# A two-layer decoder trunk: a value unit with three seven-product pairs, a key norm and the gates at later steps

## The chip, the cores and the metric

The kernel runs on one core of a Trainium2 chip. The core has TensorE (matrix products, "PE" in the profile, its weight loads "PEld"), VectorE ("DVE"), ScalarE ("ACT"), GpSimd ("POOL") and SyncE ("SP", which issues the transfers). TensorE's products go to eight PSUM banks of 128 x 512 float32; everything else lies in on-chip SBUF, and weights come from HBM. The metric is the device time of one execution in microseconds; the median of the runs is compared.

## The reference

Two layers. In each, one projection of the normed input feeds eight heads of gated linear attention (GLA) and eight heads of stick-breaking attention, whose outputs are projected back; then a squared-ReLU MLP. Sequence 256, model width 2048, float32.

```python
def hybrid_layer(x, attn_norm, w_in, w_gate_up, b_gate, gla_out_norm,
                 sb_q_norm, sb_k_norm, sb_out_norm, w_o, mlp_norm, w_up, w_down):
    h = rms_norm(x, attn_norm)
    proj = jnp.einsum('bsd,de->bse', h, w_in)
    g_q, g_k, g_v, g_gate, g_lr, s_q, s_k, s_v = jnp.split(proj, COL_SPLITS, axis=-1)
    gate_logits = jnp.einsum('bsr,re->bse', g_lr, w_gate_up) + b_gate
    log_a = jax.nn.log_sigmoid(gate_logits.astype(jnp.float32)) / GLA_GATE_TAU
    o_gla = gla_chunked(split_heads(g_q, GLA_HEADS), split_heads(g_k, GLA_HEADS),
                        split_heads(g_v, GLA_HEADS), split_heads(log_a, GLA_HEADS))
    ...
    sq = rms_norm(split_heads(s_q, SB_HEADS), sb_q_norm)
    sk = rms_norm(split_heads(s_k, SB_HEADS), sb_k_norm)
    o_sb = stick_breaking_attention(sq, sk, split_heads(s_v, SB_HEADS))
    ...
    x = x + jnp.einsum('bse,ed->bsd', mixed, w_o)
    hm = rms_norm(x, mlp_norm)
    up = jnp.square(jax.nn.relu(jnp.einsum('bsd,df->bsf', hm, w_up)))
    return x + jnp.einsum('bsf,fd->bsd', up, w_down)
```

## The kernel before

**Products in three parts.** A float32 operand is split into a high part in the reduced type float32r and a low part (the rest). A product is the sum of high x high, high x low and low x high, three matmuls on TensorE. For weights, ScalarE makes the high half (`whi`) and VectorE subtracts it from the raw weights for the low half (`wlo`); for some weights the low half is made by ScalarE and an adding transfer of GpSimd's queue (`dlo`). A raw weight tile is 1 MB and comes on SP's queue.

**A layer has two stretches.** The first is the attention (lines 811 to 1081), traced in program order and ordered by the framework. Its work is cut into units of 512 (or fewer) output columns (`unit`, line 565, and the transposed `unit_t`, line 611). Each half group of a unit's weights is followed by a call of `tick` (line 365). `after(n, fn)` (line 362) files a piece of work, and the n-th tick from then runs it, so that small pieces of TensorE's and VectorE's work are laid between the units' products. One tick is called a step below: 12 matmuls of 512 columns in `unit`, eight of 512 and eight of 256 in `unit_t`. `tick` also puts the pieces behind the newest high and low parts on their engines.

The second stretch (from line 1085) is an order written out by a planner, `Plan` (line 42): every piece has an engine, a length, predecessors, and a due time counted back from TensorE's order; VectorE and ScalarE take the piece that is due first. It holds the second gate unit ("g"), the output projection ("o"), the MLP ("up", "down"), and, in layer 1, two units of layer 2's projection, 1024 columns each: "iv" for the stick-breaking values and "ik" for the keys. They leave `natural["iv"]` and `natural["ik"]`, two tiles each, the second of which is needed by the second four heads.

**Seven-product pairs.** A unit of the planner has eight pairs of 128 weight rows, by 1024 columns. With two row tiles of the sequence and two column halves, a pair is a 2 x 2 block product. `FAST` (line 24) names the pairs that are done with seven block products in place of eight (1, 3, 5 and 6): VectorE makes sums of weight blocks (line 1097, three instructions, into `ts` and back into `raw`), sums of the operand's blocks are made once per operand pair (`forms`, line 422), and the pair has four steps (21 matmuls of 512 columns) in place of two (24). `STEPS` (line 22) is the order of the steps of a unit: the same pair number stands in it once for each step. `unit_order` (line 1109) returns both, `step_banks` (line 1119) gives the PSUM banks of each step, `steps` (line 1300) makes the weight parts. Pairs 2 and 7 (`ADDED`) take their low halves by the adding transfer.

**Layer 2's attention around the change.** The order of units is: low-rank gate columns with two query heads (line 881), the short query unit of two heads (`ub`, line 948), the long query unit of four heads (`uq`, line 964), then the GLA query and key units of `unit_t`. Steps are counted from the end of `ub`: steps 1 to 8 are `uq`, 9 to 12 the first GLA query unit, 13 to 16 the second. The pieces are:

- `sb_qk` (line 659), a norm: `head_sums` (line 642) squares a row tile and reduces it over each head (lines 645, 646), one step later `finish` does the second row tile, the inverse root, and `mul_heads` (line 651); `wait` steps after the call, `turn` transposes two heads on TensorE (line 688), and VectorE copies the result (line 695, or 697 for queries), and again one step later for two more heads. For the second key norm the input is `natural["ik"][1]`, which is normed in place.
- `sb_heads` (line 849): for the first four heads, scores at steps 2 and 6, weights (line 742) three steps and outputs (line 754) four steps later. For the second four heads, called when `uq` has ended (step 8), scores at steps 14 and 18.
- `gates` (line 903): two calls. Each has four small matmuls (line 911), ScalarE and VectorE work, a small copy on GpSimd, and three GpSimd products (line 945).

Of the kernel before, what the change touches and what calls it, by code (L numbers as in the profile page):

```python
# [21 lines left out]
STEPS = [0, 0, 1, 1, 1, 2, 3, 1, 3, 2, 3, 3, 4, 4, 5, 5, 6, 5, 5, 6, 6, 6, 7, 7]  # L22
LOADS = [0, 1, 2, 3, 4, 5, 6, 7]
FAST = (1, 3, 5, 6)
ADDED = (2, 7)
BIG = ("up", "down", "iv", "ik")
DEPTH = 2
# [117 lines left out]
def trunk_kernel(  # L145
# [51 lines left out]
    def act_tile(dt, shape=(P, 4, T)):  # L197
        return apool.tile(list(shape), dt, tag="act", name=nm("act"))

    def ps_tile():  # L200
        return pools["ps"].tile([P, 512], F32, tag="ps", name=nm("ps"))
# [8 lines left out]
    def tmp(tag, shape, dt=F32, bufs=2):  # L210
        pool = pools["att"] if tag in ATT else pools["mlp"] if tag in MLP else tpool
        return pool.tile(list(shape), dt, tag=tag, name=nm(tag), bufs=bufs)
# [20 lines left out]
    def stat(n):  # L233
        return spool.tile([P, n], F32, tag=f"st{n}", name=nm("st"))
# [127 lines left out]
    def after(n, fn):  # L362
        held.append((clock[0] + n, fn))
# [31 lines left out]
    def inv_rms(ss, n, width):  # L395
        rr, parts = inv_rms_parts(ss, n, width)
        for part in parts:
            part()
        return rr
# [19 lines left out]
    def fast(i):  # L419
        return i in FAST  # L420

    def forms(op, i, t, tag):
# [18 lines left out]
        def high():  # L441
            if e:
                if keep:
                    op.x[i] = act_tile(F32R, (P, 4, 2, P))
                else:
                    op.x[i] = tmp(tag, [P, 3, 2, P], F32R, bufs=len(FAST))
                todo.append((op.x[i], e[0]))
# [194 lines left out]
    def head_sums(ss, src, nh):  # L642

        sq = tmp("t2", [P, 512], bufs=T2)
        nc.vector.tensor_tensor(sq[:, : nh * P], src, src, ALU.mult)
        nc.vector.tensor_reduce(
            ss, sq[:, : nh * P].rearrange("p (h d) -> p h d", d=P), AX.X, ALU.add
        )

    def mul_heads(dst, src, rr, nh):  # L650
        nc.vector.tensor_tensor(
            dst.rearrange("p (h d) -> p h d", d=P),
            src.rearrange("p (h d) -> p h d", d=P),
            rr.unsqueeze(2).to_broadcast([P, nh, P]),
            ALU.mult,
        )


    def sb_qk(acc, c, nh, h0, rst, scale, dst, wait, nat=None):

        w = nh * P
        made = nat is None
        nat = act_tile(F32, (P, NT, 512)) if made else nat
        ss = stat(NT * nh)

        def part(tt):
            if made:
                nc.scalar.activation(
                    nat[:, tt, :w], acc[:, tt, c : c + w], AF.Copy, scale=rst[:, tt : tt + 1]
                )  # L670
            head_sums(ss[:, tt * nh : (tt + 1) * nh], nat[:, tt, :w], nh)

        def finish():
            part(1)
            rr = inv_rms(ss, NT * nh, P)
            for tt in range(NT):
                mul_heads(
                    nat[:, tt, :w], nat[:, tt, :w], rr[:, tt * nh : (tt + 1) * nh], nh
                )

        part(0)
        after(1, finish)

        def turn(h):
            pt = ps_tile()
            for j in range(2):
                for tt in range(NT):
                    nc.tensor.transpose(  # L688
                        pt[:, j * T + tt * P : j * T + (tt + 1) * P],
                        nat[:, tt, (h + j) * P : (h + j + 1) * P], ident,  # L690
                    )
            d = dst[:, h0 + h : h0 + h + 2, :]
            s = pt.rearrange("p (h t) -> p h t", t=T)
            if scale is None:
                nc.vector.tensor_copy(d, s)
            else:
                nc.vector.tensor_scalar(d, s, scale, None, ALU.mult)

        for i, h in enumerate(range(0, nh, 2)):
            after(wait + i, lambda h=h: turn(h))  # L700
# [86 lines left out]
    def values(acc, v):  # L787
        for tt in range(NT):
            nc.scalar.activation(
                v[:, tt, :], acc[:, tt, :], AF.Copy, scale=st["rst"][:, tt : tt + 1]  # L790
            )
        return v
# [18 lines left out]
    for l in range(DEPTH):  # L811
# [60 lines left out]
        if l == 0:  # L872
            uk = unit(hT, wl, 0, C_SK, 512)
            rst = st["rst"]
            kT = act_tile(F32)
            sb_qk(uk, 0, 4, 0, rst, None, kT, 4)
        else:
            rst = st["rst"]
            kT = act_tile(F32)
# [23 lines left out]
        def gates(b):  # L903
            if b == 0:
                gt["e"] = [act_tile(F32) for _ in range(3)]
                gt["dec"] = tmp("dec", [P, 4, 4], bufs=1)
            eb, enb, ekd = gt["e"]
            pl = ps_tile()
            for e in range(2):
                ee = 2 * b + e  # L910
                nc.tensor.matmul(
                    pl[:, e * T : (e + 1) * T], kc["wg"][:, ee * P : (ee + 1) * P], gt["lrT"],
                    start=(e == 0), stop=True, skip_group_check=True,
                )
            a = tmp("t2", [P, 512], bufs=T2)
            nc.scalar.activation(a, pl, AF.Abs)
            nc.scalar.activation(a, a, AF.Exp, scale=-1.0)
            nc.scalar.activation(a, a, AF.Ln, bias=1.0)
            nc.vector.scalar_tensor_tensor(a, pl, 0.0, a, ALU.min, ALU.subtract)
            bc = tmp("t2", [P, 512], bufs=T2)  # L920
            for e in range(2):
                es = slice(e * T, (e + 1) * T)
                nc.vector.tensor_tensor_scan(
                    bc[:, es], kc["reset"], a[:, es], 0.0, ALU.mult, ALU.add
                )
            bs = slice(2 * b, 2 * b + 2)

            def fl(t):
                return t[:, bs, :].rearrange("p e t -> p (e t)")

            nc.scalar.activation(fl(eb), bc, AF.Exp, scale=1.0 / GATE_TAU)
            nc.scalar.activation(fl(enb), bc, AF.Exp, scale=-1.0 / GATE_TAU)
            bc3 = bc.rearrange("p (n c) -> p n c", c=CHUNK)
            nc.vector.tensor_tensor(
                a.rearrange("p (n c) -> p n c", c=CHUNK),
                bc3[:, :, CHUNK - 1 : CHUNK].to_broadcast([P, 8, CHUNK]), bc3, ALU.subtract,
            )
            nc.scalar.activation(fl(ekd), a, AF.Exp, scale=1.0 / GATE_TAU)
            nc.gpsimd.tensor_copy(
                gt["dec"][:, bs, :],  # L940
                eb[:, bs, :].rearrange("p e (n c) -> p e n c", c=CHUNK)[:, :, :, CHUNK - 1],
            )
            rb = gt["row"].unsqueeze(1).to_broadcast([P, 2, T])
            for t in (eb, enb, ekd):
                nc.gpsimd.tensor_tensor(t[:, bs, :], t[:, bs, :], rb, ALU.mult)
# [3 lines left out]
        sb_qk(ub, 0, 2, 2, rst, gqk[:, l : l + 1], qT, 3)  # L949
        sb_heads(0, qT, kT, v, (2, 6))  # L950
        for b in range(2):
            after((9 if l == 0 else 1) + 2 * b, lambda b=b: gates(b))

        if l == 0:
            uv = unit(hT, wl, 0, C_SV + 512, 512)
            v = values(uv, tmp("v4", [P, NT, 512], bufs=2))
            uk = unit(hT, wl, 0, C_SK + 512, 512)
            kT = act_tile(F32)
            sb_qk(uk, 0, 4, 0, rst, None, kT, 4)
        else:  # L960
            v = natural["iv"][1]
            kT = act_tile(F32)
            after(4, lambda kT=kT: sb_qk(None, 0, 4, 0, rst, None, kT, 3, natural["ik"][1]))
        uq = unit(hT, wl, 0, C_SQ + 512, 512)
        qT = act_tile(F32)
        sb_qk(uq, 0, 4, 0, rst, gqk[:, l : l + 1], qT, 3)
# [140 lines left out]
        natural = {}  # L1107

        def unit_order(u):

            kind, _, n2 = units[u]
            if kind == "g":
                return [i // 2 for i in range(8)], ()
            if kind == "o":
                pairs = ((4, 5, 6, 7, 0, 1, 2, 3), (4, 5, 6, 0, 7, 1, 2, 3))[n2]
                return [j for j in pairs for _ in range(4 if j < 2 else 2)], (0, 1)
            return STEPS, FAST

        def step_banks(u, j, is_fast):

            kind = units[u][0]
            if kind == "g":
                return (1, 6), (1, 6)
            if kind in BIG and j in ADDED and not by_columns(u, j):
                return ((2, 4, 3, 8),) * 2
# [120 lines left out]
        def by_columns(u, i):  # L1246

            return units[u][0] in BIG and i in ADDED and i == unit_order(u)[0][-1]

# [50 lines left out]
        def steps(u, j, is_fast, r, ld, readers):  # L1300
# [23 lines left out]
            if not is_fast:  # L1324
                added = kind in BIG and j in ADDED
                if added and not by_columns(u, j):
# [292 lines left out]
        gate(0)  # L1619
        for u, (kind, q, n2) in enumerate(units):  # L1620
            order, quick = unit_order(u)
            if kind != "g":
                tails[u] = (down_tail if kind in ("o", "down") else up_tail)(u)
# [94 lines left out]
```

## Time and profile before

| | |
|---|---|
| median of 3 runs | 2145.22 us (2144.92 to 2146.12) |
| the profiled execution, its own time | 2145.51 us |
| its span, first to last instruction | 2143.8 us |
| transfers | 480.37 MB, mean 224 GB/s |
| short query unit ends on TensorE | 1188.2 us of the span |
| long query unit ends (step 8) | 1221.6 us |
| scores of step 14 begin | 1242.85 us |

All times inside the kernel are counted from the span's start. In a view of the timeline a row has the start, the duration, the engine, the line, the operation, output <- input, sizes, the count, and in brackets how long the engine stood idle before it and what released it. The time between two starts of TensorE says more than the durations, since its products overlap: a matmul of 512 columns is drawn 0.39 us long, while the next one starts 0.23 us later. The view of waits gives, for each pair of lines, the total, the number and the longest of an engine's waits.

### The profile page before, as it was taken

Reading aid. Unit: us, or ns where it says so; the run is one execution under the profiler, and the core shown is the slowest. Engines: PE = TensorE matmul, PEld = TensorE weight load, DVE = VectorE, ACT = ScalarE, POOL = GpSimd, SP = SyncE. Lnnn points to the kernel's source line nnn. Section 1 sums busy time; section 2 is a strip of 40 time slices with the busy share of each in tenths; the row PEclk is TensorE's granted clock in tenths of the full one; section 3 lists DMA queues with packets and bytes.
Section 4 is the critical chain, followed back from the end, with each engine's and each line's share of the span. In section 5 each row is a group of like instructions: output and inputs, shape, how many; then the busy total and the mean of one; then the engine's idle time right before and its main releaser. Section 6 shows DMA issues by size and latency. Waiting matters only on the chain.

```text
span 2143.8 us, 28392 instructions
## 1 busy us (share of the span) xinstructions
PE 2134.1 (100%) x10239; PEld 1780.4 (83%) x10239; DVE 1892.3 (88%) x2533; ACT 1471.4 (69%) x1889; POOL 157.0 (7%) x210
## 2 busy tenths in 40 slices
PE   9999999999999999999999999999999999999999
PEld 7988888888888888888878888888888888888887
DVE  5677669999999999999998875799999999999998
ACT  5555456678677677678776654667876776776775
POOL 0020000000000000000001200000000000000000
PEclk9999999999999999999999999999999999999999
DMA  6655456688888888888886544657888888888886
GB/s 229 196 158 167 158 197 196 196 245 265 244 253 246 260 251 243 273 236 255 238 242 170 176 159 158 202 173 228 253 243 274 236 261 247 248 247 253 255 249 182
DMA packets 169105, 480.37 MB, mean 224 GB/s; under 512 B 9370, under 2 KB 34530, under 8 KB 168964
## 3 DMA queue, kind: packets, MB, share of 16 engines
q1 hardware_dynamic: 149380, 407.24, 56.4%
q0 software_dynamic: 19584, 71.31, 17.6%
q8 instruction: 80, 1.31, 0.2%
q14 instruction: 61, 0.50, 0.1%
HBM read 405.12 MB, written 2.10 MB: 190 GB/s over the span
## 4 chain that ended last, share of the span: by engine, by line
PE 94%; DVE 3%; issue 1%; ACT 1%; DMA 0%; POOL 0%; DVEq 0%; ACTq 0%
PE acc L577 4%; PE acc L579 4%; PE acc L578 4%; PE acc L624 3%; PE acc L628 1%; DVE wlo L1268 1%; DVE wlo L560 0%; DVE xb L1097 0%; PE ps L1065 0%; DMA raw<-in_w_in_dram 0%; PE ps L1058 0%; PE ps L742 0%; PE ps L1015 0%; PE ps L688 0%; PE ps L706 0%
## 5 line engine op out<-in xcount | busy, mean ns | idle before, releaser
L1264 ACT ACTIVATE whi<-raw 128x1024 fp32r<-128x1024 f32 (+1 forms) x768 | 738.9, 976 | 314.4 <-issue 45.3
L1268 DVE TENSOR_TENSOR wlo<-raw,whi 128x1024 fp32r<-128x1024 f32 (+1 forms) x632 | 689.1, 1097 | 65.6 <-ACT whi L1264 54.0
L560 DVE TENSOR_TENSOR wlo<-raw,whi 128x1024 fp32r<-128x1024 f32 (+2 forms) x162 | 182.2, 1131 | 93.3 <-ACT whi L558 93.2
L558 ACT ACTIVATE whi<-raw 128x1024 fp32r<-128x1024 f32 (+2 forms) x162 | 156.0, 968 | 153.4 <-PE acc L579 109.3
L1277 POOL DMA_DIRECT2D dlo<-raw x136 | 117.2, 862 | 1587.6 <-ACT dlo L1274 837.7
L1264 ACT ACTIVATE whi<-ts 128x1024 fp32r<-128x1024 f32 x144 | 152.7, 1061 | 73.6 <-DVE ts L1097 4.0
L577 PE MATMUL acc<-whi,act 128*128 128x512 f32 (+2 forms) x512 | 191.4, 374 | 0.0
L578 PE MATMUL acc<-wlo,act 128*128 128x512 f32 (+2 forms) x512 | 186.5, 364 | 0.1
L579 PE MATMUL acc<-whi,act 128*128 128x512 f32 (+2 forms) x512 | 186.5, 364 | 0.0
L1268 DVE TENSOR_TENSOR wlo<-ts,whi 128x1024 fp32r<-128x1024 f32 x144 | 175.5, 1219 | 10.2 <-ACT whi L1264 8.5
L1097 DVE TENSOR_TENSOR ts<-raw 128x1024 f32<-128x1024 f32 x144 | 175.6, 1220 | 1.6
L1274 ACT ACTIVATE dlo<-raw 128x1024 fp32r<-128x1024 f32 x136 | 139.0, 1044 | 3.6 <-PE m__1930_9320 L1378 1.7
L577 PEld LDWEIGHTS acc<-whi,act 128*128 128x128 f32 x512 | 96.7, 189 | 17.5 <-issue 2.7
L579 PEld LDWEIGHTS acc<-whi,act 128*128 128x128 f32 x512 | 96.4, 188 | 15.5
L578 PEld LDWEIGHTS acc<-wlo,act 128*128 128x128 f32 x512 | 96.6, 189 | 14.2 <-DVE wlo L560 0.6
L1097 DVE TENSOR_TENSOR raw<-raw 128x512 f32<-128x512 f32 x144 | 98.9, 687 | 2.3
L1097 DVE TENSOR_TENSOR raw<-ts,raw 128x512 f32<-128x512 f32 x144 | 98.6, 684 | 0.5
L624 PE MATMUL acc<-act,whi 128*128 128x512 f32 x256 | 91.9, 401 | 0.0
L628 PE MATMUL acc<-act,wlo 128*128 128x256 f32 x256 | 71.6, 280 | 0.0
L1469 ACT ACTIVATE act<-act,st 128x512 f32<-128x512 f32 x72 | 49.0, 712 | 19.2 <-DVE act L1097 19.2
L454 DVE TENSOR_TENSOR act<-t,act 128x512 fp32r<-128x512 f32 x84 | 57.0, 683 | 0.0
L624 PEld LDWEIGHTS acc<-act,whi 128*128 128x128 f32 x256 | 48.1, 188 | 10.7
(3145 smaller groups left out, 5333.1 us busy)
## 6 DMA issues: line engine op xcount, KB each, us to landing
raw<-in_w_up_dram SPq DMA_DIRECT2D x112, 1024.0 KB, 5.7
raw<-in_w_down_dram SPq DMA_DIRECT2D x112, 1024.0 KB, 5.9
raw<-in_w_in_dram SPq DMA_DIRECT2D x82, 1024.0 KB, 5.3
dlo<-raw POOLq DMA_DIRECT2D x136, 512.0 KB, 6.5
raw<-in_w_o_dram SPq DMA_DIRECT2D x32, 1024.0 KB, 5.1
raw<-in_w_up_dram SPq DMA_DIRECT2D x32, 512.0 KB, 6.3
raw<-in_w_down_dram SPq DMA_DIRECT2D x32, 512.0 KB, 6.5
raw<-in_w_in_dram SPq DMA_DIRECT2D x18, 512.0 KB, 5.9
```

What stands on the lines that cost most here:

```text
L558: newest["hi"] = nc.scalar.activation(h, r, AF.Copy).ins
L560: newest["lo"] = nc.vector.tensor_tensor(lo[:, q : q + step, :width], r, f32(h), ALU.subtract).ins
L577: nc.tensor.matmul(o, xh[:, sl], whi[:, j, :width], start=first, stop=False)
L578: nc.tensor.matmul(o, xh[:, sl], wlo[:, j, :width], start=False, stop=False)
L579: st["mm"] = nc.tensor.matmul(o, xl[:, sl], whi[:, j, :width], start=False, stop=last).ins
L624: nc.tensor.matmul(acc[:, f, :], whi[:, j, sl], op.both(k), start=(k == 0), stop=False, skip_group_check=True,)
L628: nc.tensor.matmul(acc[:, f, T:], wlo[:, j, sl], xh, start=False, stop=(k == KT - 1), skip_group_check=True,)
L1097: nc.vector.tensor_tensor(dst, a, b, op)
L1264: nc.scalar.activation(box["h"][:, :n], src(), AF.Copy)
L1268: nc.vector.tensor_tensor(box["l"][:, :n], src(), f32(box["h"][:, :n]), ALU.subtract)
L1274: nc.scalar.activation(box["l"], src(), AF.Copy, scale=-1.0)
L1277: nc.gpsimd.dma_start(f32(box["l"]), src(), accum_op=ALU.add)
```

## The change

Three edits, all for layer 1's unit "iv" and layer 2's attention.

```diff
+FEWER = [0, 0, 1, 1, 1, 2, 3, 1, 3, 2, 3, 3, 4, 4, 5, 5, 6, 6, 6, 6, 7, 7], (1, 3, 6)
...
         for b in range(2):
-            after((9 if l == 0 else 1) + 2 * b, lambda b=b: gates(b))
+            after((9 if l == 0 else 2) + 2 * b, lambda b=b: gates(b))
...
-            after(4, lambda kT=kT: sb_qk(None, 0, 4, 0, rst, None, kT, 3, natural["ik"][1]))
+            after(10, lambda kT=kT: sb_qk(None, 0, 4, 0, rst, None, kT, 2, natural["ik"][1]))
...
-            return STEPS, FAST
+            return FEWER if kind == "iv" else (STEPS, FAST)
```

In the unit "iv" the pairs 1, 3 and 6 have seven products; pair 5 is plain and has two steps, directly behind pair 4's, and pair 6's four steps follow one another. All other units of the planner, "ik" among them, keep `STEPS` and `FAST`, and `forms` still makes the operand's sums for pair 5, which "ik" reads. In layer 2, the second key norm begins at step 10 (it was 4), ends at step 11 (5), and turns its heads at steps 12 and 13 (7 and 8). The two calls of `gates` come at steps 2 and 4 (1 and 3); at step 2 they stand behind the scores of that step, which are filed first.

## The prediction

> **What bounds the kernel now.** I read the page first, then the waits of TensorE around the places that the diff touches, then those places instruction by instruction.
>
> ```profile
> span 2143.8 us, 28392 instructions
> PE 2134.1 (100%) x10239; PEld 1780.4 (83%) x10239; DVE 1892.3 (88%) x2533; ACT 1471.4 (69%) x1889; POOL 157.0 (7%) x210
> ```
>
> TensorE is busy for the whole span, so the time changes only by products added to or taken from it and by moments in which it waits. Between 980 and 1400 us (the end of layer 1 and the attention of layer 2) the view of waits, for TensorE, has three rows (total us, times, longest):
>
> ```profile
> PE ps L688 <- DVE act L651: 1.9, 2, 1.6
> PE m__2025_9760 L1378 <- DVE wlo L1268: 0.6, 1, 0.6
> PE m__2028_9771 L1378 <- DVE wlo L1268: 0.5, 1, 0.5
> ```
>
> All three waits are for VectorE, and all three lie where the diff works: L1268 makes the low halves for the value unit "iv", L651 ends the second key norm of layer 2. The stretches around them, engine by engine (PE, PEld, DVE, ACT, POOL busy us, each with its count):
>
> ```profile
> 1100.00:1116.00 16.00, 14.85 (x63) 11.24 (x62) 15.93 (x22) 12.16 (x17) 1.72 (x2) 1.00 0.89 239
> 1216.00:1222.00 6.00, 4.09 (x22) 3.17 (x21) 5.90 (x14) 4.54 (x7) 0.00 (x0) 1.00 0.89 286
> ```
>
> VectorE is full in both (15.93 of 16, 5.90 of 6) and TensorE is not. The granted clock is 1.00 in both, so these are waits, not a slower clock.
>
> **Part 1: pair 5 of the value unit becomes a plain pair.** The end of that unit on TensorE now, from pair 5's first product to pair 7's first:
>
> ```profile
> 1104.71 0.39 PE L1377 MATMUL m__2001_9660<-whi,act 128*128 128x512 f32 x1
> ...
> 1108.80 0.39 PE L1377 MATMUL m__2028_9771<-whi,act 128*128 128x512 f32 x1
> 1109.65 0.50 PE L1378 MATMUL m__2028_9771<-wlo,act 128*128 128x512 f32 x1 [0.46 <-DVE wlo L1268]
> ...
> 1111.60 0.40 PE L1377 MATMUL m__2025_9760<-whi,act 128*128 128x512 f32 x1
> 1112.59 0.50 PE L1378 MATMUL m__2025_9760<-wlo,act 128*128 128x512 f32 x1 [0.59 <-DVE wlo L1268]
> ...
> 1116.32 0.40 PE L1377 MATMUL m__2001_9660<-whi,act 128*128 128x512 f32 x1
> ```
>
> Between the first two rows lie three steps of six matmuls: 4.09 us / 18 = 0.227 us each, the undisturbed cadence. From 1104.71 to 1116.32 there are two seven-product pairs of 21 matmuls, 42 x 0.227 = 9.53 us, but the stretch takes 11.61: 2.08 us are lost. After the change it holds one plain pair (two steps x two banks x two blocks x three products, 24 matmuls) and one fast pair (21): 45 x 0.227 = 10.22 us. The three matmuls cost 0.68 us; if every wait goes, the stretch is 1.39 us shorter.
>
> Does every wait go? VectorE's groups between 1080 and 1120 us give the prices (the mean ns stands last before the idle column):
>
> ```profile
> L1268 DVE TENSOR_TENSOR wlo<-raw,whi 128x1024 fp32r<-128x1024 f32 x11 | 13.4, 1218 | 0.8 <-ACT whi L1264 0.8
> L1097 DVE TENSOR_TENSOR ts<-raw 128x1024 f32<-128x1024 f32 x4 | 4.9, 1218 | 0.0
> L1268 DVE TENSOR_TENSOR wlo<-ts,whi 128x1024 fp32r<-128x1024 f32 x4 | 4.9, 1216 | 0.0
> L1097 DVE TENSOR_TENSOR raw<-ts,raw 128x512 f32<-128x512 f32 x5 | 3.4, 683 | 0.0
> L1268 DVE TENSOR_TENSOR wlo<-raw,whi 128x512 fp32r<-128x512 f32 x4 | 2.7, 684 | 0.0
> L1097 DVE TENSOR_TENSOR raw<-raw 128x512 f32<-128x512 f32 x4 | 2.7, 683 | 0.0
> ```
>
> A fast pair takes the three weight sums (1.22 + 0.68 + 0.68) and four low parts (1.22 + 1.22 + 1.22 + 0.68): 6.9 us. A plain pair takes two low parts, 2.4 us. VectorE is relieved of 4.5 us, more than twice the 2.08 us by which it comes late, and pair 6, whose four steps now stand together (6.9 us of VectorE against 21 x 0.227 = 4.8 us of TensorE), has plain pairs 4 and 5 ahead of it (48 x 0.227 = 10.9 us of TensorE for 4.9 us of VectorE). So the waits should go. Ends: nothing gained and 0.68 us paid, or 1.39 us gained. I take 1.25, since behind 1109.98 the matmuls followed each other at 0.23 to 0.24 us even where nothing waited, and that may stay. What is not saved: the operand sums of pair 5 are still made, because the key unit "ik" keeps four fast pairs. Eight loads stay eight, ScalarE loses two high parts, no queue gets a new transfer. The ring of high tiles is two places further on when layer 2 begins; each place is freed in the same order, so I cost that at nothing.
>
> **Part 2: the second key norm leaves steps 4 to 8 behind the short query unit.** (A step is one tick, a half group of weights.) VectorE there:
>
> ```profile
> 1201.50 2.26 DVE L560 TENSOR_TENSOR wlo<-raw,whi 128x1024 fp32r<-128x1024 f32 x1 [0.87 <-ACT whi L558]
> ...
> 1207.66 0.67 DVE L645 TENSOR_TENSOR t<-act 128x512 f32<-128x512 f32 x1
> ...
> 1208.85 0.68 DVE L646 TENSOR_REDUCE st<-t 128x4 f32<-128x512 f32 x1
> 1209.44 1.47 DVE L645 TENSOR_TENSOR t<-act 128x512 f32<-128x512 f32 x1
> 1210.83 2.29 DVE L560 TENSOR_TENSOR wlo<-raw,whi 128x1024 fp32r<-128x1024 f32 x1
> 1213.05 0.67 DVE L646 TENSOR_REDUCE st<-t 128x4 f32<-128x512 f32 x1
> 1213.64 1.71 DVE L560 TENSOR_TENSOR wlo<-raw,whi 128x1024 fp32r<-128x1024 f32 x1
> ...
> 1216.49 0.16 DVE L389 TENSOR_TENSOR st<-st 128x8 f32<-128x8 f32 x1
> ...
> 1217.08 1.29 DVE L651 TENSOR_TENSOR act<-act,st 128x512 f32<-128x512 f32 x2
> ```
>
> And TensorE, which stands at the first transposes of that key tile:
>
> ```profile
> 1215.80 0.39 PE L579 MATMUL acc<-whi,act 128*128 128x512 f32 x1
> 1217.83 0.33 PE L688 MATMUL ps<-ident,act 128*128 128x128 f32 x1 [1.64 <-DVE act L651]
> ...
> 1218.73 0.47 PE L577 MATMUL acc<-whi,act 128*128 128x512 f32 x1
> ...
> 1221.57 0.60 PE L688 MATMUL ps<-ident,act 128*128 128x128 f32 x4
> 1221.92 0.48 PE L624 MATMUL acc<-act,whi 128*128 128x512 f32 x1
> ```
>
> The undisturbed block of four transposes takes 0.35 us (1221.57 to 1221.92). The disturbed one takes from 1215.80 + 0.23 to 1218.73, 2.70 us: 2.35 us lost. The norm's place is free of other necessity: its input was there since the end of layer 1, its result is first read by the scores of step 14. So this loss goes, and the eight transposes themselves (0.7 us) only change place.
>
> What comes late next is the question. The new place is steps 10 to 13, beside the norm of the long query unit:
>
> ```profile
> 1230.74 1.29 DVE L651 TENSOR_TENSOR act<-act,st 128x512 f32<-128x512 f32 x2
> ...
> 1234.61 0.74 DVE L697 TENSOR_SCALAR act<-ps,gqk 128x512 f32<-128x512 f32 x1
> ```
> ```profile
> 1233.07 0.60 PE L688 MATMUL ps<-ident,act 128*128 128x128 f32 x4
> 1236.33 0.60 PE L688 MATMUL ps<-ident,act 128*128 128x128 f32 x4
> ```
>
> That query norm ends at 1232.03, 1.04 us before step 11's turn (1233.07) needs it. The move takes from VectorE ahead of this point 0.67 + 0.68 + 1.47 + 0.67 + 1.29, four small instructions like L389 (0.16 each, 0.6) and the two copies behind the turns (0.74 each, by L697): 6.9 us. TensorE comes sooner by 2.35 + 0.70 = 3.05 us. If VectorE does all the key norm ahead of the query's, it takes on 0.67 x 4 + 0.6 + 1.29 = 4.6 us again: 1.04 + 6.9 - 4.6 - 3.05 = 0.3 us to spare. If it does the query's first, the key's turns at step 12 (behind 1236.33) meet a norm that ends about as late. That is close to even, and VectorE cannot bring all 6.9 us forward, because much of its work waits for TensorE's results. So a new wait in L688 has the ends 0 and the 2.35 us of the old one; I take 0.4, nearer the end that the ledger gives. Queued behind such a turn would be the rest of the first GLA query unit; VectorE's copies and the scores of step 14 wait for it. The moved step issues no transfer; SP's queue of weight loads keeps its order. Each turn needs one of four "ps" banks and step 14 two; the copies that free them (0.7 us) have a step of about 3.2 us (1233.07 to 1236.33). The natural key tile is held five steps longer and the key tile taken five steps later, so only steps 12 and 13 want one more of the 17 "act" buffers, when the query's natural tile is being freed.
>
> **Part 3: gates a step later.** Nothing is added: TensorE's gate products follow the scores of step 2 instead of going ahead of them. The result is first multiplied behind step 12, so the step is covered; without cover it would cost one step, 2.7 us (12 x 0.227). The six GpSimd products are moved with it:
>
> ```profile
> L945 POOL TENSOR_TENSOR act<-act,row x6: 1273/1453/2272, 1198.6 to 1212.0; 128x512 f32<-128x512 f32 x6
> ```
>
> Beside them the rows above show four VectorE instructions with two inputs in SBUF drawn out: 2.26, 2.29 and 1.71 instead of 1.22, and 1.47 instead of 0.67, in all 1.04 + 1.07 + 0.49 + 0.80 = 3.4 us. I take the same 3.4 us a step later, so nothing; ends are 0 and all six at 1.45 us, 8.7. The Trainium skill (SBUF — State Buffer, "Who interferes with whom") says that such a VectorE instruction and a GpSimd instruction that reads SBUF exclude one another, the later blocked to the end of the earlier. By that rule the worst is the end of 8.7 us, since any six instructions can be met; the rows so far show less than half of it.
>
> **Sum.** -1.25 - 2.35 + 0.4 = -3.2 us. The profiled execution took 2145.51 us (span 2143.8), 0.29 above the median of the runs, 2145.22. From its own time 2142.3, set against the median 2142.0.
>
> **Rivals.**
> - *Everything goes, the slow cadence too, and no new wait* (0.24): -1.39 - 2.35 = -3.74, 2141.5. For it: VectorE's relief of 4.5 us in part 1 is large; against it: the close ledger of part 2.
> - *The wait moves with the norm* (0.12): a new wait in L688 at step 12 of the old size, 2.35. Then only part 1 is left, 2145.22 - 1.25 = 2144.0. For it: VectorE's ledger leaves 0.3 us.
> - *The value unit doesn't gain* (0.08; the change does not do what it says): pair 6 alone still asks 6.9 us of VectorE for 4.8 us of TensorE, and if its parts are ordered late, 0.68 us are paid and waits of the old size stay: 0.68 - 2.35 + 0.4 = -1.3, 2143.9. Against it: 10.9 us of plain pairs ahead.
> - *Slower* (0.12): the GpSimd products, moved to steps 3 to 7, each hold a two-input VectorE instruction for their whole 1.45 us: 8.7 instead of 3.4 us, VectorE 5.3 us later. Less the 0.3 us to spare, step 11's turn waits 5.0 us instead of 0.4: -1.25 - 2.35 + 5.0 = +1.4, 2146.6. It decides as soon as that wait exceeds 3.6 us. It is the case that the skill's rule allows.
> - The forecast holds the rest, 0.44.
>
> **How the numbers follow.** The forecast's own range is 2141.3 to 2143.2. 2140.2 to 2145.2 holds the forecast, the first three rivals and the runs' scatter (2144.92 to 2146.12 before), and leaves out the slower one and a little below. 0.2% of 2145.2, about what a measurement can tell from no change, is 4.3 us: below 2140.9 or above 2149.5. My best case stops at 2141.5; that relief of VectorE gains something I do not see in its rows, part of the first rival and a little of the forecast, makes 0.18 for faster. Slower by 4.3 us needs a wait of 7.9 us in part 2: most of the slower rival's chance ends short of that, 0.08. Same: 0.74.
>
> **What would show it.** Right: TensorE's waits list between 980 and 1400 us without L1378 <- wlo and with L688 <- L651 under 1 us; about 10.2 to 10.4 us from pair 5's first product to pair 7's; L651 of the key norm ended before TensorE's second query turn. Wrong: a wait in L688 of 2 us or more near 1230 us, rows of L742 or L706 (scores) waiting for copies, low parts L1268 still late in pair 6, or VectorE instructions of over 2 us beside L945 in more than three places.

## The result, and the profile after

| | before | after |
|---|---|---|
| median of 22 runs each | 2145.97 us (2144.80 to 2147.50) | 2143.01 us (2142.38 to 2143.59) |
| the profiled execution, its own time | 2145.51 us | 2143.19 us |
| its span | 2143.8 us | 2141.5 us |

The ratio is 0.9986, with a 95% interval of 0.9979 to 0.9992: 0.14% faster, in the range 2140.2 to 2145.2 and, by the bound of 0.2%, "same". In the kernel after, every line behind line 25 has a number one higher: the norm's last step is L652, its transposes L689, the value unit's products L1378 and L1379. The head of the page of after:

```profile
span 2141.5 us, 28382 instructions
PE 2132.6 (100%) x10242; PEld 1779.8 (83%) x10242; DVE 1886.6 (88%) x2528; ACT 1470.5 (69%) x1887; POOL 158.4 (7%) x210
```

Three products more on TensorE, five instructions fewer on VectorE, two fewer on ScalarE: the edit of part 1. The waits of TensorE between 980 and 1400 us (total us, times, longest):

```profile
PE ps L689 <- DVE act L652: 0.8, 1, 0.8
PE m__2011_9701 L1379 <- DMA dlo<-raw: 0.3, 1, 0.3
```

The three old rows are gone (L688 1.9; L1378 0.6 and 0.5). Two new ones are there: a smaller wait of the transposes, and one for a low half that comes by an adding transfer. The timeline of TensorE in after, at both places:

```profile
1104.54 0.39 PE L1378 MATMUL m__2001_9660<-whi,act 128*128 128x512 f32 x1
...
1114.74 0.39 PE L1378 MATMUL m__2001_9660<-whi,act 128*128 128x512 f32 x1
...
1117.46 0.39 PE L1378 MATMUL m__2011_9701<-whi,act 128*128 128x512 f32 x1
1118.11 0.50 PE L1379 MATMUL m__2011_9701<-dlo,act 128*128 128x512 f32 x1 [0.26 <-DMA dlo<-raw]
...
1161.54 0.28 PE L578 MATMUL acc<-whi,act 128*128 128x272 f32 x1
...
1235.35 0.40 PE L625 MATMUL acc<-act,whi 128*128 128x512 f32 x1
1236.50 0.41 PE L689 MATMUL ps<-ident,act 128*128 128x128 f32 x2 [0.75 <-DVE act L652]
1236.74 0.38 PE L778 MATMUL ps<-ident,on 128*128 128x128 f32 x2
1237.01 0.87 PE L689 MATMUL ps<-ident,act 128*128 128x128 f32 x6
...
1240.15 0.59 PE L707 MATMUL ps<-act,act 128*128 128x256 f32 x2
```

In the value unit, pair 5's first product to pair 7's first (the first two rows) takes 10.20 us instead of 11.61: no wait is left in it, and no slow cadence. Behind it the product with `dlo` starts 0.65 us after the one ahead of it instead of 0.23: 0.42 us lost. At the key's turn, the last product starts at 1235.35 and the first transpose 1.15 us later instead of 0.23: 0.92 us lost. The framework put both turns of the key together here (eight transposes of L689), next to transposes of the output norm (L778).

Two fixed points cut the gain into three. Before they lie here, the first product of the low-rank unit and the scores of step 14:

```profile
1162.60 0.28 PE L577 MATMUL acc<-whi,act 128*128 128x272 f32 x1
...
1242.85 0.59 PE L706 MATMUL ps<-act,act 128*128 128x256 f32 x2
```

| stretch | before, us | after, us | difference |
|---|---|---|---|
| start to the low-rank unit | 1162.60 | 1161.54 | -1.06 (-1.41 in the value unit, +0.42 the `dlo` wait, -0.07 other) |
| low-rank unit to the scores of step 14 | 80.25 | 78.61 | -1.64 |
| the rest of the span | 900.95 | 901.35 | +0.40 |
| sum | 2143.8 | 2141.5 | -2.3 |

The middle stretch is the place of parts 2 and 3, and the measure for the experiments below: -2.35 for the old wait, +0.92 for the new one, and -0.2 elsewhere. From one execution to the next it moves by some tenths: two later profiles of the kernel before, with the same wait of the transposes, have 80.35 and 80.63.

### The profile page after: what moved, and what is told of

The parts are those of the page before. It is cut to its first block, busy times and chain, and to the rows that moved or that the text cites. A ratio compares the mean times of both kernels' runs of the same rounds, so it can differ in the third digit from the quotient of the medians.

```text
span 2141.5 us, 28382 instructions
## 1 busy us (share of the span) xinstructions
PE 2132.6 (100%) x10242; PEld 1779.8 (83%) x10242; DVE 1886.6 (88%) x2528; ACT 1470.5 (69%) x1887; POOL 158.4 (7%) x210
## 4 chain that ended last, share of the span: by engine, by line
PE 95%; DVE 2%; issue 1%; DMA 1%; ACT 1%; POOL 0%; ACTq 0%; DVEq 0%; POOLq 0%
PE acc L578 5%; PE acc L580 5%; PE acc L579 5%; PE acc L625 2%; PE acc L629 1%; DMA dlo<-raw 1%; DVE wlo L561 0%; DVE xb L1098 0%; PE ps L1066 0%; PE ps L1059 0%; DVE wlo L1269 0%; PE ps L689 0%; PE ps L1016 0%; PE ps L707 0%; PE ps L743 0%
## 5 line engine op out<-in xcount | busy, mean ns | idle before, releaser
L561 DVE TENSOR_TENSOR wlo<-raw,whi 128x1024 fp32r<-128x1024 f32 (+2 forms) x162 | 179.8, 1116 | 96.6 <-ACT whi L559 96.4
L1269 DVE TENSOR_TENSOR wlo<-ts,whi 128x1024 fp32r<-128x1024 f32 x143 | 174.4, 1220 | 10.2 <-ACT whi L1265 8.5
```

Source lines behind the costliest of these rows:

```text
L561: newest["lo"] = nc.vector.tensor_tensor(lo[:, q : q + step, :width], r, f32(h), ALU.subtract).ins
L1269: nc.vector.tensor_tensor(box["l"][:, :n], src(), f32(box["h"][:, :n]), ALU.subtract)
```

## The experiments

Each edit is shown against the kernel before unless said otherwise. All compute the same result: only the order of work and the number of seven-product pairs differ. Kernels of one group shared chip and runs of the kernel before. The ratio of a kernel to the kernel before stands with its 95% interval in brackets; where the interval reaches 1, the waits in the trace carry the argument, not the time.

**First group: each part by itself.** The kernel before had a median of 2145.92 us over 33 runs (2145.09 to 2148.03).

*Only the pairs* (with the line of `FEWER`, as in the change):

```diff
-            return STEPS, FAST
+            return FEWER if kind == "iv" else (STEPS, FAST)
```

> Only the value unit's edit (FEWER for iv), norm and gates as before. Theory, the three edits act in separate places and add up: the stretch from pair 5's first product to pair 7's is 10.2 us as in the changed kernel (11.6 before), the late dlo of pair 7 costs TensorE about 0.4 us there, and the 2.3 us in front of line 688/689's turn at step 7 stay, so about 1.0 us under the kernel before. Rival, the relief in the value unit gives VectorE a head start that also shortens the wait at step 7: about 2 us or more under before, with the step-7 wait clearly under 1.6 us.

Measured: 2144.98 us (2143.47 to 2146.46), ratio 0.9994 [0.9985, 1.0003], so -0.94. Its waits of TensorE in the same window:

```profile
PE ps L689 <- DVE act L652: 1.7, 2, 1.5
PE m__2011_9701 L1379 <- DMA dlo<-raw: 0.3, 1, 0.3
```

The waits for `wlo` are gone without the other parts, and the old wait of the transposes stays. What follows: part 1 takes its waits away alone, and the `dlo` wait belongs to it. The time agrees with the -1.0 expected, but the interval reaches over 1.

*Only the norm:*

```diff
-            after(4, lambda kT=kT: sb_qk(None, 0, 4, 0, rst, None, kT, 3, natural["ik"][1]))
+            after(10, lambda kT=kT: sb_qk(None, 0, 4, 0, rst, None, kT, 2, natural["ik"][1]))
```

> Only the second key norm's edit (start at step 10, turns at 12 and 13), pairs and gates as before. Theory: the 2.3 us at step 7 go, a new wait of about 0.9 us in front of the key's turn as in the changed kernel comes, so about 1.4 to 1.8 us under before; the gates' place does not matter. Rival, the gates' later step is what leaves VectorE free: with the gates at steps 1 and 3 the GpSimd products draw out 3.4 us of VectorE as before instead of the 1.5 to 2 of the changed kernel, the new wait is 2 us or more and the time is within 0.5 us of before.

Measured: 2143.41 us (2142.80 to 2144.50), 0.9988 [0.9979, 0.9997], so -2.5, more than I expected. Its waits:

```profile
PE m__2025_9760 L1378 <- DVE wlo L1268: 0.6, 1, 0.6
PE ps L742 <- DVE hl L731: 0.5, 1, 0.5
PE m__2028_9771 L1378 <- DVE wlo L1268: 0.4, 1, 0.4
```

No wait of the transposes is left in this view: with the gates in their old place the norm's move brings no new wait at the key's turn. The wait of L742 (TensorE's products for the attention weights) is no sign of the move: two later profiles of the kernel before have it too, 0.4 and 0.2 us.

*Only the gates:*

```diff
-            after((9 if l == 0 else 1) + 2 * b, lambda b=b: gates(b))
+            after((9 if l == 0 else 2) + 2 * b, lambda b=b: gates(b))
```

> Only the gates' edit (steps 2 and 4), pairs and key norm as before. Theory: the gates by themselves gain nothing, the key norm's wait at step 7 stays at 2 us or is longer by up to 1 us, since the gates' VectorE work now lies even nearer to it: within 1 us of before, not faster by more than 0.5. Rival: the VectorE instructions beside the GpSimd products are drawn out by 1.5 us less, and the wait at step 7 shrinks by that: 1 to 1.5 us under before.

Measured: 2149.46 us (2147.09 to 2150.12), 1.0015 [1.0006, 1.0024], so +3.5: a miss of mine. Its first wait:

```profile
PE ps L688 <- DVE act L651: 3.4, 1, 3.4
```

The old wait, 1.9 us in before, has grown by 1.5 us. The rest of the 3.5 goes with TensorE's clock (last section). Part 3 is not free: VectorE comes to the key norm later when the gates do.

*Norm and gates, the pairs as before:*

> Both edits of the attention, the value unit as before. Theory: additive, so the change (2.9 us under before) less the value unit's 1.0: about 1.9 us under before, with the new wait of 0.9 us at the key's turn and the waits of 0.6 and 0.5 us of line 1378 in the value unit as before. Rival, the value unit's relief is needed for it: the new wait at the key's turn is longer than 1.5 us and less than 1.2 us are gained.

Measured: 2144.49 us (2143.97 to 2144.85), 0.9991 [0.9983, 1.0000], so -1.4 where 1.9 was expected. The wait of the transposes is back, the same as in the change:

```profile
PE ps L688 <- DVE act L651: 0.8, 1, 0.8
```

Against the norm alone the gates cost 2144.49 - 2143.41 = 1.1 us, and the value unit has no part in that wait.

**Second group: is it the turn's place, VectorE's work, or the gates?** The kernel before had 2145.81 us over 33 runs (2144.88 to 2147.79).

*Only the turn late*, the norm's work at step 4 as before, its transposes at steps 12 and 13:

```diff
-            after(4, lambda kT=kT: sb_qk(None, 0, 4, 0, rst, None, kT, 3, natural["ik"][1]))
+            after(4, lambda kT=kT: sb_qk(None, 0, 4, 0, rst, None, kT, 8, natural["ik"][1]))
```

> The kernel before with only the turns of the second key norm later (norm still begins at step 4, turns at 12 and 13 in place of 7 and 8); pairs and gates as before. Theory, TensorE's loss is the turn standing in its queue ahead of a norm that is not ready, so the late turn alone takes the 2.3 us away and needs no move of VectorE's work: about 2 us under before, no wait of line 688 over 0.4 us. Rival, VectorE's work between steps 4 and 8 is itself the bound, and with the norm left there its lateness shows at the next reader (scores or weights at steps 5 to 9, the query's turn at step 11) with 1 us or more: at most 1 us under before.

Measured: 2147.17 us (2146.53 to 2147.42), 1.0005 [0.9996, 1.0014]. The waits have moved, not gone:

```profile
PE ps L777 <- DVE on L651: 1.7, 1, 1.7
PE ps L688 <- DVE act L651: 1.3, 1, 1.3
...
PE ps L742 <- DVE hl L731: 0.2, 1, 0.2
```

VectorE still does the norm in steps 4 to 8, and now the output norm (`on`) and the query norm behind it are late. It is the rival that held. So the gain of part 2 needs the work to leave steps 4 to 8 of VectorE; that TensorE asks later is not enough.

*The change with the norm a step earlier:*

```diff
-            after(10, lambda kT=kT: sb_qk(None, 0, 4, 0, rst, None, kT, 2, natural["ik"][1]))
+            after(9, lambda kT=kT: sb_qk(None, 0, 4, 0, rst, None, kT, 3, natural["ik"][1]))
```

> The change with the key norm begun one step sooner (step 9) and the turns where they are (12 and 13). Theory, VectorE is full from 1214 to 1240 us, so the same work ends no sooner: the wait of 0.9 us stays at the key's turn or comes up at the query's turn, within 0.4 us of the change. Rival, it is only the order, the norm's end was filed too late: the wait goes and 0.7 to 0.9 us are gained on the change.

Measured: 2143.10 us (2142.36 to 2143.66), 0.9986 [0.9978, 0.9995], as the change. The timeline of TensorE shows that the wait sits at the query's turn instead:

```profile
1228.71 0.33 PE L689 MATMUL ps<-ident,act 128*128 128x128 f32 x1 [0.54 <-DVE act L652]
```

The query's norm ends later on VectorE, since work of the key's norm now lies among its own; first in the change, then here:

```profile
1226.70 1.28 DVE L652 TENSOR_TENSOR act<-act,st 128x512 f32<-128x512 f32 x2
```
```profile
1227.97 1.28 DVE L652 TENSOR_TENSOR act<-act,st 128x512 f32<-128x512 f32 x2
```

VectorE is full here (25.80 of the 26 us from 1214 to 1240), so what the key's norm gains, the query's norm loses.

*The change with plain pair 5 in "ik" too:*

```diff
-            return FEWER if kind == "iv" else (STEPS, FAST)
+            return FEWER if kind in ("iv", "ik") else (STEPS, FAST)
```

> The change with FEWER for the key unit ik as well as for iv, where no wait was seen before. Theory, a plain pair costs three matmuls of 0.227 us and gains only where VectorE is late: 0.7 us slower than the change (the operand sums of pair 5 are made but read by none). Rival, VectorE's relief is carried into layer 2's attention and shortens the wait at the key's turn: same as the change or faster.

Measured: 2143.76 us (2143.23 to 2144.95), 0.9991 [0.9982, 1.0000]: 0.75 us over the change (across groups), near the 3 x 0.227 = 0.68 of its three products. In the traces the low-rank unit begins at 1161.58, against 1160.96 to 1161.06 in the three other profiles with the pairs and without a `dlo` wait: 0.5 to 0.6 us later. Where TensorE does not wait, a plain pair only costs.

*The change with the gates back in their old place* (pairs and norm only):

```diff
-            after((9 if l == 0 else 2) + 2 * b, lambda b=b: gates(b))
+            after((9 if l == 0 else 1) + 2 * b, lambda b=b: gates(b))
```

> Pairs and key norm as in the change, gates back at steps 1 and 3. Theory, the gates' later step only changes where VectorE is late (it takes 0.6 us of wait from line 743 at step 5 and puts 0.9 us in front of the key's turn): 0.3 to 1.0 us faster than the change, that is about 3.3 to 3.9 us under the kernel before, with a wait of line 743 near 1205 us of about 0.4 to 0.6 us and under 0.4 us in front of the key's turn. Rival, with the value unit's relief VectorE is ahead and the gates' place does not matter at all: within 0.3 us of the change.

Measured: 2142.07 us (2141.51 to 2142.77), 0.9982 [0.9973, 0.9991], span 2139.9. It is below both kernels, 1.03 us under the late gates with the norm at 9 in the same group (which differs in the norm's step too), and no row is left in its waits of TensorE between 980 and 1400 us; the 0.4 to 0.6 us of line 743 that I expected did not come. (Its interval overlaps that of the change, 0.9979 to 0.9992. That it is faster than the change rests on the runs, of which only 5 of the change's 22 lie under the slowest of these 11, on the middle stretch and on the other pairs that differ in the gates alone, next table.) The timeline of TensorE at the key's turn and the scores:

```profile
1235.12 0.39 PE L625 MATMUL acc<-act,whi 128*128 128x512 f32 x1
1235.35 0.41 PE L689 MATMUL ps<-ident,act 128*128 128x128 f32 x2
...
1238.65 0.59 PE L707 MATMUL ps<-act,act 128*128 128x256 f32 x2
```

The first transpose follows at the undisturbed 0.23 us. The low-rank unit began at 1160.97, so the middle stretch is 77.68 us, 0.93 less than in the change.

**Third group.** The kernel before had 2145.72 us over 15 runs (2144.72 to 2147.35).

*As the last, with the norm at step 9* (both edits above together):

> Pairs as in the change, gates at steps 1 and 3, key norm begun at step 9 instead of 10, turns at 12 and 13. Theory: with the gates early nothing waits in this stretch any more, so a sooner norm gains nothing: within 0.4 us of the kernel with pairs and norm and without the gates' edit (2142.07). Rival: the norm's work one step sooner stands ahead of the query's norm and the query's turn at step 11 waits, 0.5 to 1 us slower than that.

Measured: 2142.48 us (2141.40 to 2143.44), 0.9984 [0.9975, 0.9993], and no wait either: 0.41 us over the last, across groups, at the edge of the 0.4 expected, and no sign of the rival's wait. Three more profiles are of the kernel before by itself:

> The kernel before, unchanged, for one more profile, because its times fall in two groups (near 2145.5 and near 2147.2 us) and the changed kernel's do not. Theory: in the upper group the wait of about 2 us in front of line 688 is followed by a stretch of 3.4 us at half the granted clock, as in the profile of the pairs alone, 1.7 us; the profile shows that stretch if its time is above 2146.5 us and does not if it is below 2146. Rival: the groups have nothing to do with the clock, and a profile above 2146.5 us shows 1.00 throughout.

> The same again: with the half clock behind the wait near 1220 us if above 2146.5 us, without it if below 2146.

> The kernel before once more, since both profiles so far fell into the lower group and showed 1.00: with the half clock behind the wait near 1220 us if above 2146.5 us, without it if below 2146.

Measured: 2145.97, 2145.51 and 2147.06 us, the third on another chip than the first two; they serve the last section.

What the gates' late place costs, wherever two kernels differ in it alone:

| the rest | gates early, us | gates late, us | cost |
|---|---|---|---|
| pairs and norm as before | 2145.92 | 2149.46 | 3.5 |
| norm at 10, pairs as before | 2143.41 | 2144.49 | 1.1 |
| pairs and norm at 10 | 2142.07 | 2143.01 | 0.9 |
| pairs and norm at 9 | 2142.48 | 2143.10 | 0.6 |

The first two rows are within a group, the last two across groups.

**Why the late gates cost time.** VectorE in the 50 us from the long query unit's first products to the key's turn, first after, then with the gates early (the unit begins at 1187.10 and 1186.53, so the windows are laid 0.5 us apart). Columns: length, then the busy time of PE, PEld, DVE, ACT and POOL, each with its count, granted clock, transfer share, GB/s:

```profile
1186.50:1216.50 30.00, 30.00 (x153) 24.68 (x152) 24.23 (x38) 23.72 (x39) 11.28 (x8) 1.00 0.62 197
1216.50:1236.50 20.00, 19.25 (x119) 16.86 (x117) 19.88 (x41) 12.30 (x21) 1.25 (x3) 1.00 0.34 104
```
```profile
1186.00:1216.00 30.00, 30.00 (x153) 24.62 (x153) 26.11 (x37) 24.09 (x38) 11.07 (x8) 1.00 0.60 193
1216.00:1236.00 20.00, 20.00 (x125) 17.65 (x124) 19.86 (x42) 11.72 (x22) 1.04 (x2) 1.00 0.37 116
```

Behind 1216 us VectorE is full in both. Ahead of it VectorE stands idle for 5.77 us with late gates and 3.89 with early ones. What it stands idle for, with late gates, its three longest idle times in this window:

```profile
1197.24 0.69 DVE L727 SCALAR_TENSOR_TENSOR ha<-ps,ha 128x512 f32<-128x512 f32 x1 [2.00 <-ACT ha L726]
...
1206.66 1.51 DVE L561 TENSOR_TENSOR wlo<-raw,whi 128x1024 fp32r<-128x1024 f32 x1 [1.98 <-ACT whi L559]
...
1213.43 0.86 DVE L646 TENSOR_TENSOR t<-on 128x512 f32<-128x512 f32 x1 [1.12 <-ACT on L768]
```

With early gates, pieces of the first call of `gates` (L920, L924, L935) run where the first of these idle times lies, and the longest idle time is one for TensorE:

```profile
1193.38 0.68 DVE L920 SCALAR_TENSOR_TENSOR t<-ps,t 128x512 f32<-128x512 f32 x1
1194.10 1.27 DVE L924 TENSOR_TENSOR_SCAN t<-reset,t 128x256 f32<-128x256 f32 x2
...
1196.40 0.68 DVE L935 TENSOR_TENSOR t<-t 128x512 f32<-128x512 f32 x1
1198.24 0.75 DVE L698 TENSOR_SCALAR act<-ps,gqk 128x512 f32<-128x512 f32 x1 [1.16 <-PE ps L689]
1199.54 2.27 DVE L561 TENSOR_TENSOR wlo<-raw,whi 128x1024 fp32r<-128x1024 f32 x1 [0.55 <-ACT whi L559]
```

By all such rows VectorE waits 5.5 us for ScalarE in this window with late gates, and 2.6 us, with 1.2 us for TensorE, with early ones. That the gates' pieces would have filled the longer idle times is read from these rows; no run tests it apart. In return less is drawn out beside GpSimd's products, taken together 1.4 us with late gates and 2.8 us with early ones: a low part (L561) takes 1.22 us elsewhere, and three of them take 2.27, 1.79 and 1.79 us with early gates, one 1.51 us with late ones. So of the 1.9 us by which the idle time grew, some 0.5 us are missing for good (an estimate: 1.9 - 1.4), and from 1216 us on VectorE has no idle time in which to make them up. The end of the key norm on VectorE, after and then with early gates:

```profile
1235.67 1.28 DVE L652 TENSOR_TENSOR act<-act,st 128x512 f32<-128x512 f32 x2
```
```profile
1234.52 1.28 DVE L652 TENSOR_TENSOR act<-act,st 128x512 f32<-128x512 f32 x2
```

It is 1.15 us later, 0.58 of that beyond the 0.57 by which the whole unit begins later. TensorE reaches the turn 0.34 us sooner there, counted the same way (1235.35 - 1235.12 = 0.23 later, less 0.57). 0.58 + 0.34 = 0.92 us: the new wait.

## Why the prediction was right, point by point

**Part 1, -1.25 taken.** Right in mechanism and size: 10.20 us, the lower end of the 10.2 to 10.4 that should show it, so -1.41, and the slow cadence that I left in did not stay. VectorE's relief was enough. Not foreseen: TensorE, now sooner, meets pair 7's adding transfer, 0.42 us in the profile of after and 0.49 in that of the pairs alone, but not in the four other profiles with the pairs (the norm at 9, "ik" too, and the two with early gates): a transfer that lands at varying times. Net -1.06 in the profile and -0.94 in the runs of the pairs alone.

**Part 2, -2.35 + 0.4 taken.** The old loss went whole. The new wait is 0.92 us, inside the ends 0 and 2.35, and above the 0.4 I took. My ledger, 0.3 us to spare, was worked out for the other order, with the key's norm first, so it was not put to the test; that there is no wait with the gates early agrees with its closeness and no more. The sign that I named did not hold: the key norm's last instructions lie behind the query's second turn, not ahead of it. VectorE did the query's norm first, the order that I gave as the other one, and the key's turn then met a norm that "ends about as late", as the prediction says.

**Part 3, nothing taken.** This is the step that failed: "I take the same 3.4 us a step later, so nothing". It priced the gates by what their GpSimd products draw out, and by when their result is needed. What it left out is that VectorE has idle time early in the stretch and none later: the idle time that the moved work no longer fills is not made up. The four pairs of kernels price it at 0.6 to 1.1 us, and at 3.5 us where the key norm stayed in steps 4 to 8. The new wait of part 2 goes with this cost, not with the norm's move: it is there in the profiles with late gates and a late norm, and in none of the three with early gates and a late norm.

**The slower rival** (GpSimd's products hold VectorE, 2146.6) fell. In after GpSimd's six products are these:

```profile
1203.67 5.65 POOL L946 TENSOR_TENSOR act<-act,row 128x512 f32<-128x512 f32 x3
...
1212.44 4.26 POOL L946 TENSOR_TENSOR act<-act,row 128x512 f32<-128x512 f32 x3
```

They last 9.9 us together (9.3 in before, where the prediction took six times the median, 8.7), and beside them VectorE's instructions are drawn out by about 1.4 us, less than the 3.4 of before. By the rule of the Trainium skill (SBUF — State Buffer, "Who interferes with whom"), that the two exclude one another, up to all 9.9 us could have been lost, as an estimate; the rows show 1.4. How much is lost depends on which instructions meet, and the kernel with early gates is the faster one although 2.8 us are drawn out in it.

**The other rivals.** "The wait moves with the norm" held for 0.92 of 2.35 us, and through the gates. "The value unit doesn't gain" fell. "Everything goes, no new wait" (2141.5) is nearly what pairs and norm without the gates' edit give, 2142.07.

**The sum.** -3.2 us was predicted; the profiles differ by 2.3 and the medians by 2.96. By terms against the profile: part 1 -1.25 against -1.06, parts 2 and 3 -1.95 against -1.64, and 0.40 us in the rest of the span that I did not predict. That 0.40 lies without a long wait of TensorE behind step 14. Part of it is scatter: three later profiles of the kernel before have 900.99 to 901.15 us there, against the 900.95 of the first. The cause of the rest stays open. The medians differ by more because some executions of the kernel before also lose time by TensorE's clock (last section). So that 2.96 lies near 3.2 is partly luck: the prediction did not count the clock, and without it the gain is about 2.6. The time itself, 2143.01, is 1.0 us over the 2142.0 of the forecast, near the upper end of its own range, 2143.2.

## What to carry to other kernels

When an engine is full over a long stretch, the order of its work decides who waits. The key norm went from one full part of VectorE to another: in before, VectorE was busy for 13.58 of the 14 us from 1204 to 1218, where the norm was, and for 13.72 of the 14 us from 1226 to 1240, where it is now. It paid all the same, because work that is needed sooner no longer stood behind it; the run with only the turn late bears that out. Moving small work from an idle moment into the full stretch costs time for what it leaves idle, here about 0.6 to 1.1 us, however late its result is needed. So for every edit that is "covered" because nobody needs its result yet, look at what the engine does at the old place and at the new one, not at the due time alone. And price each part of a combined edit with the others in place: here two gained 1 and 2.5 us and the third took back about 0.9. Alone the third cost 3.5, so the three taken alone add up to +0.1 us, while together they gain 2.96.

## What the runs showed of the hardware that was not expected

A wait of TensorE of 1.5 us can be followed by a drop of its granted clock, which cost 1.6 us more. Of the three later profiles of the kernel before, all with nearly the same wait of the transposes, the one of 2147.06 us has the drop, those of 2145.97 and 2145.51 have not. The windows of the third profile and of the first (granted clock is the third number from the end):

```profile
1216.00:1220.00 4.00, 2.18 (x10) 1.62 (x10) 3.90 (x10) 2.74 (x6) 0.00 (x0) 0.94 1.00 311
1220.00:1224.00 4.00, 4.00 (x15) 3.15 (x15) 3.77 (x9) 2.85 (x6) 0.00 (x0) 0.64 0.27 95
```
```profile
1216.00:1220.00 4.00, 2.12 (x11) 1.35 (x10) 3.90 (x9) 2.94 (x6) 0.00 (x0) 1.00 0.99 311
1220.00:1224.00 4.00, 4.00 (x24) 3.40 (x23) 3.93 (x10) 3.49 (x7) 0.00 (x0) 1.00 0.35 123
```

And TensorE in the third profile, behind the wait:

```profile
1217.69 0.33 PE L688 MATMUL ps<-ident,act 128*128 128x128 f32 x1 [1.55 <-DVE act L651]
1218.29 0.55 PE L688 MATMUL ps<-ident,act 128*128 128x128 f32 x3 [0.27 <-DVE act L651]
...
1219.68 0.63 PE L578 MATMUL acc<-wlo,act 128*128 128x512 f32 x1
1220.11 0.63 PE L579 MATMUL acc<-whi,act 128*128 128x512 f32 x1
1220.54 0.63 PE L577 MATMUL acc<-whi,act 128*128 128x512 f32 x1
```

The products follow each other at 0.43 us instead of 0.227 for about 3.4 us, at half the clock (0.50 in the window 1220 to 1222.5), some 1.6 us lost: from the first product behind the transposes to the first behind the next four transposes it is 4.79 us, and 3.19 in the first profile of before, which has no drop. The idle time ahead of it is 1.55 + 0.27 us. The Trainium skill (TensorE: Matmul & The Clock Gate, "HAM oscillation — how this bites in real kernels") gives as the rule that no gap in TensorE's work be longer than about 3.4 us; here the drop came behind a gap of about half of that, in some executions and not in others. The mean granted clock of each run shows how often:

| kernel | runs at a mean clock of 1.000 | runs below it |
|---|---|---|
| before, three groups | 55 of 81, medians 2145.45 to 2145.67 us | 26 of 81, medians 2147.08 to 2147.32 us |
| pairs alone (wait 1.5 us) | 6 of 11, 2144.42 us | 5 of 11, 2145.84 us |
| gates alone (wait 3.4 us) | 1 of 11, 2147.09 us | 10 of 11, 2148.28 to 2150.12 us (0.998 in six of them, 0.999 in the others and in the rows above) |
| the three with a wait of 0.8 us (the change; norm and gates; "ik" too) | 44 of 44 | none |
| the four with less or none (norm alone; norm at 9; gates early, twice) | 44 of 44 | none |

At full clock the change gains about 2145.6 - 2143.0 = 2.6 us (an estimate across groups); the rest of the 2.96 is the chance of the drop, which goes with the wait. The gates alone cost 1.5 us at full clock, by the one run that had it (2147.09 against 2145.62); that the rest of their 3.5 is the drop is read from the mean clocks, since only one of the ten runs below full clock was profiled. The turn placed late, with waits of 1.7 and 1.3 us, had the lower mean in 2 of 11 runs without a longer time, so the wait's length alone does not decide it; what does is open.
